# A two-layer decoder trunk on one core: scores negated as they are read, weight splits held back, first FFN sums ahead of splits

## The chip, the cores and the metric

The kernel runs on one NeuronCore of a Trainium2 chip. Its engines work side by side, each through its own queue in order: TensorE (PE, with its weight loads shown as PEld), VectorE (DVE), ScalarE (ACT), GpSimd (POOL) and SyncE (SP), which here only issues loads. The metric is device time in microseconds (us) of one launch. The order in each queue is fixed when the program is built: the builder lets a simulated clock run and gives each engine, at each moment, the earliest written instruction that is ready by that clock. On the chip an engine then takes its list from the front, and waits where the front is not ready.

## The reference

Two layers; each is half-step SwiGLU, token mixing, half-step SwiGLU, all on x of 256 rows and 1024 columns in float32, and a last RMS norm. Cut to what matters:

```python
def swiglu(x, w_gate, w_up, w_down):
    return (jax.nn.silu(x @ w_gate) * (x @ w_up)) @ w_down      # D_FF = 2816

def masked_softmax(s, valid):
    s = jnp.where(valid, s.astype(jnp.float32), NEG)
    m = jnp.max(s, axis=-1, keepdims=True)
    p = jnp.where(valid, jnp.exp(s - m), 0.0)
    return p / jnp.maximum(jnp.sum(p, axis=-1, keepdims=True), 1.0)

for l in range(DEPTH):                                           # DEPTH = 2
    x = x + 0.5 * swiglu(rms_norm(x, norm_ffn1[l]), ...)
    x = x + hybrid_mixer(rms_norm(x, norm_mix[l]), ...)          # 8 NSA heads, 8 MoBA heads
    x = x + 0.5 * swiglu(rms_norm(x, norm_ffn2[l]), ...)
return rms_norm(x, norm_final)
```

At 256 rows every block of keys is chosen, so each NSA head needs two softmaxes over causal scores (selected and window keys) and one over 15 compressed keys, and each MoBA head one.

## The kernel before, in words

**Exact products.** Every weight is used as two numbers, hi and lo, with hi + lo the float32 weight, and x likewise. Weights come as a stream of blocks of 128 x 1024, in the order of use (class `Stream`). SP loads a block into one of 5 raw buffers (`wraw`, line 236); ScalarE casts it to `whi` (line 260); VectorE subtracts to `wlo` (line 290). That is a *split*. There are 7 buffers for split blocks, freed when the last matmul of a block is done. A raw buffer is free, and SP's next load can start, when its `wlo` is written.

**When splits are written.** `split(n)` writes n of them if buffers are free; `pump()` writes splits until only `st.reserve` of the 7 buffers are left. `use()` takes the next block. Since the builder gives an engine whatever is ready first, `st.behind["V"]` and `st.behind["A"]` name an instruction of VectorE or ScalarE behind which all splits written from then on have to stand on that engine (`queue`, with `tc.issue_after`).

**FFN.** 22 blocks j of 128 hidden columns. For each, 8 pairs of matmuls for the gate and 8 for the up product (`wide`, lines 594 and 596: the first of a pair reads `whi`, the second `wlo`) go to two PSUM banks: tag B (two banks) for even j, C and D for odd j. `read(j)` (line 676) takes both banks: ScalarE copies one half of a bank (line 680), VectorE adds the other (line 681); then the bank is free. `finish(j)` multiplies by the norm's scale on GpSimd (line 689), applies silu on ScalarE, multiplies again on GpSimd (line 691), and splits the result. Down products (lines 572 to 574) follow later. At the start of an FFN (but for the first one) j = 0 and j = 1 are computed together (`gu_two`), then `read(0)`, `read(1)` and `st.split(2)` are written, then j = 2, which needs the B banks again. There are three such starts. When the matmuls of j = 0 and 1 begin, their four blocks hold four of the 7 buffers, and the blocks of j = 2 and 3 are the next to be split.

**Mixer.** Projections run as blocks `mk`, `mq` (two for each half of the MoBA heads), `mv` and `out`; `m_feat`, `m_v` and `part` use one block each and pump. Between them stand the heads' softmaxes. `nsa_s(h)` computes scores in PSUM (line 1101), and `softmax` reads them: for each of two branches VectorE scales, masks and stores the scores and reduces them to their maximum in one instruction (lines 1046, 1047; the accumulator read behind it writes `mx`), one small VectorE instruction turns the sign (`nm`, line 1049), and ScalarE computes the exponentials with `nm` as bias and their sums (lines 1051, 1052). `normalize` takes the reciprocals on VectorE and multiplies P on GpSimd (lines 1066, 1067); `nsa_t` turns P on TensorE (line 1074, into tag A) and ScalarE copies it out (`PT`, line 1076); `nsa_pv` multiplies by the values (line 1084). MoBA heads go the same way with one branch. The keys' and queries' rotation runs over ScalarE (line 820), two small transfers, VectorE and GpSimd (lines 826, 827); `m_stack` splits the turned keys (`KM`, line 1163).

Of the kernel before, what the change touches and what calls it, by code (L numbers as in the profile page):

```python
# [21 lines left out]
F32 = mybir.dt.float32  # L22
# [3 lines left out]
AF = mybir.ActivationFunctionType  # L26
OP = mybir.AluOpType
AX = mybir.AxisListType

D, S, L, DH = 1024, 256, 2, 64  # L30
# [51 lines left out]
def all_units(phases):  # L82
    return [u for ph, l in phases for u in phase_units(ph, l)]
# [234 lines left out]
def trunk(ctx, tc, xin, wst, w1st, gains, glast, cst, small, out, phases=PHASES, n_raw=5, n_hl=7):  # L318
    nc = tc.nc
    V, A, G, T = nc.vector, nc.scalar, nc.gpsimd, nc.tensor  # L320
# [3 lines left out]
    mp = ctx.enter_context(tc.tile_pool(name="mix", bufs=1))  # L324
# [3 lines left out]
    st = Stream(nc, wst, all_units(phases), rawp, hlp, n_raw, n_hl)  # L328
# [10 lines left out]
    def bank(tag):  # L339
        return ps.tile([128, 512], F32, name="ps" + tag, tag="ps" + tag, bufs=BUFS[tag])  # L340
# [24 lines left out]
    def con(n):  # L365
        a, c = CONST_AT[n]
        return cs_t[:, a:a + c]
# [27 lines left out]
    def half_of(h):  # L395
        return slice(h * 512, (h + 1) * 512)
# [18 lines left out]
    def x_add(h, o):  # L415
# [5 lines left out]
        for t in range(2):  # L421
            q = mp.tile([128, 512], F32, name="sqt", tag="P", bufs=3)
            A.activation(q, X[:, t, half_of(h)], AF.Square, accum_out=state["sq"][:, h, t:t + 1])
# [24 lines left out]
    def x_start_squares():  # L448
        sq = state["sq"] = mp.tile([128, 2, S], F32, name="sqacc", tag="P", bufs=3)
        with tc.issue_after(state["second_hi"]):  # L450
            A.activation(sq, XF[:, :2], AF.Square)
            for d in range(2, KT, 2):
                q = mp.tile([128, 2, S], F32, name="sqt", tag="P", bufs=3)
                A.activation(q, XF[:, d:d + 2], AF.Square)
                G.tensor_add(sq, sq, q)
        G.tensor_add(sq[:, 0], sq[:, 0], sq[:, 1])
# [6 lines left out]
    def last_add(t, n, o):  # L463
# [6 lines left out]
        V.tensor_add(x, x, o)  # L470
        q = mp.tile([128, 512], F32, name="sqt", tag="P", bufs=3)
        A.activation(q[:, :b - a], x, AF.Square, accum_out=sq[:, t, n:n + 1])
# [171 lines left out]
    def ffn(pi, name, l):  # L644
# [31 lines left out]
        def read(j):  # L676

            s = S_[j] = mp.tile([128, 2, S], F32, name="hs", tag="PT", bufs=5)
            for i, o in enumerate(pend.pop(j)):
                A.copy(s[:, i], o[:, S:])  # L680
                V.tensor_add(s[:, i], s[:, i], o[:, :S])  # L681

        def finish(j):
            n = 0 if j == NJ - 1 else 1
# [15 lines left out]
        def evac(j):  # L700
            read(j)
            finish(j)
# [101 lines left out]
    def mixer(pi, l):  # L804
# [95 lines left out]
        rotk = rawk[:, 2:4]  # L900
        rs = state["rs"]
        rs8 = mp.tile([128, 2], F32, name="rs8", bufs=2)
        nrs = mp.tile([128, 2], F32, name="nrs", bufs=2)
        G.tensor_scalar(rs8, rs, DH ** -0.5, None, op0=OP.mult)
        A.activation(warm, rs8[:, 0:1], AF.Exp, scale=0.0)
        G.tensor_scalar(nrs, rs, -1.0, None, op0=OP.mult)
# [86 lines left out]
        def c_scores():  # L993
            b = bank("A")
            for blk in range(2):
                for r in range(4):
                    c = (blk * 4 + r) * 32
                    T.matmul(b[:, c:c + 32], rawq[:, r, blk * 128:(blk + 1) * 128], KC, start=True, stop=True)
            P = mp.tile([128, 2, 8, 16], F32, name="Pc", bufs=1)
            m = mp.tile([128, 2, 8], F32, name="mc", bufs=1)  # L1000
            for blk in range(2):
                V.scalar_tensor_tensor(P[:, blk], b[:, blk * 128:(blk + 1) * 128].rearrange("p (h n) -> p h n", h=8),
                                       rs8[:, blk:blk + 1],
# [32 lines left out]
        m0, m1 = con("mask")[:, 128:], con("mask")  # L1036

        def softmax(key, s1, s0, nb, gates):

            P = mp.tile([128, 3, 2, 128], F32, name="P", tag="P", bufs=3)[:, :, :nb]  # L1040
            m = mp.tile([128, 2, nb], F32, name=f"mx{nb}", bufs=3)
            nm = mp.tile([128, 2, nb], F32, name=f"nm{nb}", bufs=3)
            sm = mp.tile([128, 2, nb], F32, name=f"sm{nb}", bufs=3)
            mk = m1.rearrange("p (k t) -> p k t", k=2)
            for r in range(nb):
                V.tensor_tensor_reduce(P[:, 0:2, r], s1[:, :, r], mk, rs8[:, 1:2], -3e38, OP.add, OP.max, m[:, 0, r:r + 1])
                read = V.tensor_tensor_reduce(P[:, 2, r], s0[:, r], m0, rs8[:, 0:1], -3e38, OP.add, OP.max,
                                              m[:, 1, r:r + 1]).ins
            V.tensor_scalar(nm, m, -1.0, None, op0=OP.mult)
            for r in range(nb):  # L1050
                A.activation(P[:, 0:2, r], P[:, 0:2, r], AF.Exp, bias=nm[:, 0, r:r + 1], accum_out=sm[:, 0, r:r + 1])
                e = A.activation(P[:, 2, r], P[:, 2, r], AF.Exp, bias=nm[:, 1, r:r + 1], accum_out=sm[:, 1, r:r + 1]).ins
            if gates is not None:
                st.behind["A"] = e
            PR[key] = (P, sm, nb, gates)
            return read
# [12 lines left out]
        def transpose_p(key, tag):  # L1069
            P, _, nb, _ = PR.pop(key)  # L1070
            for r in range(nb):
                b = bank(tag)
                for o, s in ((0, 2), (1, 0), (2, 1)):
                    last = T.transpose(b[:, o * 128:(o + 1) * 128], P[:, s, r], ident).ins
                t = mp.tile([128, 384], F32, name="PT", tag="PT", bufs=5)
                cur["copied"] = A.copy(t, b[:, :384]).ins
                PT[key, r] = t
            return last
# [30 lines left out]
        def nsa_t(h):  # L1109
            transpose_p(h, "A")  # L1110
# [23 lines left out]
        def m_feat(which, i):  # L1134
            if i == 0:
                cur["rot"] = RW("rot" + which)
            if i % 2 == 0:
                cur["b"] = bank("A")
            cur["last"] = feature_one(cur["b"][:, (i % 2) * S:(i % 2 + 1) * S], st.use("in", l, i), i % 2 == 0)
            if i % 2 == 1:  # L1140
                h = i // 2
                raw = mp.tile([128, 2, S], F32, name="mraw", tag="F", bufs=2)
                tabs = (CK, SK) if which == "mk" else (con("C"), con("Sg"))
                sw, ro = SW[:, 2 * h:2 * h + 2], cur["rot"][:, 2 * h:2 * h + 2]
                rope_begin(cur["b"], raw, sw, ro, tabs[0])
                ends.append((which, h, sw, ro, tabs[1]))
            st.pump()
# [90 lines left out]
        normalize(5)  # L1238
        m_end()
        nsa_s(6)  # L1240
        st.reserve = 2
        m_feat("mq", 2)
        nsa_pv(1)
        nsa_t(4)
# [1 line left out]
        m_stack()  # L1246
        nsa_s(7)
        nsa_t(5)
        m_feat("mq", 3)


# [55 lines left out]
        nsa_t(6)  # L1307
        normalize(("m", 0))
        moba_s(1)
        st.reserve = 1  # L1310
        st.behind.clear()
        m_v(1)
        nsa_t(7)
# [12 lines left out]
                 (moba_s, 7), (part, 3, 0), (normalize, ("m", 6)), (moba_pv, 2), (part, 3, 1), (moba_t, 6), (part, 4, 0),  # L1326
                 (normalize, ("m", 7)), (moba_t, 7), (part, 4, 1), (moba_pv, 3)]
        for f, *args in steps:
            if args == [4, 0]:
                st.reserve = 0  # L1330
            with tc.issue_after(last):
                last = f(*args) or last
        st.reserve = 1
# [30 lines left out]
    for pi, (ph, l) in enumerate(phases):  # L1364
        if ph == "mix":
            mixer(pi, l)
        else:
            ffn(pi, ph, l)
# [36 lines left out]
```

## Time and profile before

| | us |
|---|---|
| median of three runs (1019.35 to 1098.41) | 1021.62 |
| profiled execution | 1018.07 |
| its span, first to last instruction | 1016.3 |
| PE busy in it | 996.7 (98%) |
| DVE busy | 698.2 (69%) |
| ACT busy | 592.6 (58%) |
| POOL busy | 323.0 (32%) |

The mean granted clock of TensorE was 0.997 of full speed. The first mixer runs from about 191 to 322 us, the second from about 691 to 821; the three FFN starts in question lie at about 338, 523 and 837 us. Read the table for how little room each engine leaves, and then the stages one by one: a share of the whole span hides that VectorE is nearly full in the middle of a mixer.

### The profile page before, as it was taken

Reading aid. Unit: us, or ns where it says so; the run is one execution under the profiler, and the core shown is the slowest. Engines: PE = TensorE matmul, PEld = TensorE weight load, DVE = VectorE, ACT = ScalarE, POOL = GpSimd, SP = SyncE. Lnnn points to the kernel's source line nnn. Section 1 sums busy time; section 2 is a strip of 40 time slices with the busy share of each in tenths; the row PEclk is TensorE's granted clock in tenths of the full one; section 3 lists DMA queues with packets and bytes.
Section 4 is the critical chain, followed back from the end, with each engine's and each line's share of the span. In section 5 each row is a group of like instructions: output and inputs, shape, how many; then the busy total and the mean of one; then the engine's idle time right before and its main releaser. Section 6 shows DMA issues by size and latency. Waiting matters only on the chain.

```text
span 1016.3 us, 16192 instructions
## 1 busy us (share of the span) xinstructions
PE 996.7 (98%) x5873; PEld 861.8 (85%) x5873; DVE 698.2 (69%) x1195; ACT 592.6 (58%) x1137; POOL 323.0 (32%) x412
## 2 busy tenths in 40 slices
PE   9999999999899999999999999999999999999997
PEld 7888888899778888888888888889987788888885
DVE  6876566689984866666676656666899757666664
ACT  6755555557864855555575555456578756555552
POOL 2322122136751322222242222131477313222220
PEclk9999999999999999999999999999999999999999
DMA  8786776354452666666557677863436427666631
GB/s 275 249 292 198 266 251 214 105 171 149 130 166 84 213 205 193 195 188 189 164 186 207 188 232 231 280 189 125 158 110 185 132 84 252 198 212 187 189 123 42
DMA packets 52848, 188.21 MB, mean 185 GB/s; under 512 B 6368, under 2 KB 6752, under 8 KB 51616
## 3 DMA queue, kind: packets, MB, share of 16 engines
q1 hardware_dynamic: 49680, 182.17, 56.5%
q10 hardware_dynamic: 3088, 5.01, 1.8%
q8 instruction: 46, 0.75, 0.3%
q14 instruction: 34, 0.28, 0.1%
HBM read 182.04 MB, written 1.05 MB: 180 GB/s over the span
## 4 chain that ended last, share of the span: by engine, by line
PE 91%; DVE 4%; ACT 2%; issue 1%; POOL 1%; DMA 1%; ACTq 0%; POOLq 0%; DVEq 0%
PE psB L594 16%; PE psA L572 9%; PE psA L574 9%; PE psA L573 9%; PE psB L596 8%; PE psC L594 8%; PE psD L594 8%; PE psD L596 4%; PE psC L596 4%; PE psA L565 2%; PE psA L566 2%; PE psA L567 2%; PE psA L407 1%; PE psD L1084 1%; DVE wlo L290 1%
## 5 line engine op out<-in xcount | busy, mean ns | idle before, releaser
L290 DVE TENSOR_TENSOR wlo<-wraw,whi 128x1024 fp32r<-128x1024 f32 x325 | 411.1, 1272 | 208.7 <-ACT whi L260 208.3
L260 ACT CAST whi<-wraw 128x1024 fp32r<-128x1024 f32 (+1 forms) x326 | 337.7, 1044 | 276.3 <-issue 172.1
L594 PE MATMUL psB<-x,whi 128*128 128x512 f32 x688 | 242.4, 393 | 1.1 <-DVE hs L681 1.1
L689 POOL TENSOR_TENSOR hs<-hs,rbc 128x256 f32<-128x256 f32 x88 | 76.5, 871 | 400.7 <-DVE hs L681 366.5
L596 PE MATMUL psB<-x,wlo 128*128 128x256 f32 x688 | 192.6, 280 | 0.0
L594 PEld LDWEIGHTS psB<-x,whi 128*128 128x128 f32 x688 | 129.2, 188 | 30.0 <-DVE hs L681 1.9
L574 PE MATMUL psA<-wlo,hp 128*128 128x512 f32 (+1 forms) x356 | 137.6, 387 | 0.0
L573 PE MATMUL psA<-whi,hp 128*128 128x512 f32 (+1 forms) x356 | 137.5, 387 | 0.0
L572 PE MATMUL psA<-whi,hp 128*128 128x512 f32 (+1 forms) x356 | 137.0, 388 | 0.5 <-DVE X L470 0.5
L596 PEld LDWEIGHTS psB<-x,wlo 128*128 128x128 f32 x688 | 129.4, 188 | 1.4
L691 POOL TENSOR_TENSOR hs<-hs,rbc 128x256 f32<-128x256 f32 x88 | 101.8, 1160 | 72.2 <-ACT hs L690 72.0
L594 PE MATMUL psC<-x,whi 128*128 128x512 f32 x344 | 122.0, 392 | 0.0
L594 PE MATMUL psD<-x,whi 128*128 128x512 f32 x344 | 121.7, 391 | 0.0
L596 PE MATMUL psC<-x,wlo 128*128 128x256 f32 x344 | 96.2, 280 | 0.0
L596 PE MATMUL psD<-x,wlo 128*128 128x256 f32 x344 | 96.2, 280 | 0.0
L572 PEld LDWEIGHTS psA<-whi,hp 128*128 128x128 f32 x356 | 66.8, 188 | 14.3 <-DVE X L470 0.7
L574 PEld LDWEIGHTS psA<-wlo,hp 128*128 128x128 f32 x356 | 66.8, 188 | 13.7
L573 PEld LDWEIGHTS psA<-whi,hp 128*128 128x128 f32 x356 | 66.9, 188 | 12.2
L594 PEld LDWEIGHTS psD<-x,whi 128*128 128x128 f32 x344 | 64.6, 188 | 14.3
L594 PEld LDWEIGHTS psC<-x,whi 128*128 128x128 f32 x344 | 64.6, 188 | 14.1
L565 PE MATMUL psA<-x,whi 128*128 128x256 f32 x256 | 73.0, 285 | 0.0
L567 PE MATMUL psA<-x,wlo 128*128 128x256 f32 x256 | 72.3, 282 | 0.0
(245 smaller groups left out, 1599.8 us busy)
## 6 DMA issues: line engine op xcount, KB each, us to landing
wraw<-in_w SPq DMA_DIRECT2D x318, 512.0 KB, 4.3
W1a<-in_w SPq DMA_DIRECT2D x4, 1024.0 KB, 6.2
W1mixn<-in_w SPq DMA_DIRECT2D x2, 1024.0 KB, 6.4
W1late<-in_w SPq DMA_DIRECT2D x2, 1024.0 KB, 5.9
KM<-KM ACTq DMA_DIRECT2D x8, 256.0 KB, 3.8
wraw<-in_w SPq DMA_DIRECT2D x4, 420.0 KB, 3.1
wraw<-in_w SPq DMA_DIRECT2D x4, 256.0 KB, 4.8
X<-in_small SPq DMA_DIRECT2D x1, 1024.0 KB, 7.3
```

Of the source, the lines that this page charges most:

```text
L260: self.last_hi = self.nc.scalar.copy(hi[:, a:b], raw[:, a:b]).ins
L290: eng.tensor_sub(lo[:, :c], raw[:, :c], hi[:, :c].bitcast(F32))
L565: T.matmul(o, hi, xh, start=first, stop=False, skip_group_check=True)
L566: T.matmul(o, hi, xl, start=False, stop=False, skip_group_check=True)
L567: return T.matmul(o, lo, xh, start=False, stop=last, skip_group_check=True).ins
L572: T.matmul(o, parts[:, 0, c], hi, start=first, stop=False, skip_group_check=True)
L573: T.matmul(o, parts[:, 1, c], hi, start=False, stop=False, skip_group_check=True)
L574: return T.matmul(o, parts[:, 0, c], lo, start=False, stop=last, skip_group_check=True).ins
L594: T.matmul(o, blk128(hi, k), x.rearrange("p a t -> p (a t)"), start=k == 0, stop=k == KT - 1, skip_group_check=True)
L596: last = T.matmul(o[:, S:], blk128(lo, k), x[:, 0], start=False, stop=k == KT - 1, skip_group_check=True).ins
L689: G.tensor_mul(g, g, state["rbc"])
L691: G.tensor_mul(g, g, state["rbc5"])
```

## The change

Three parts. The score scale is negated (a new small tile `nrs8`, one GpSimd instruction per mixer), the reduction takes the minimum, so that it writes minus the maximum, and the exponential takes scale -1; the 32 `nm` instructions go. The reserve of split buffers stays 3 through the block `mq 2` instead of `mk 3`; in the `mv` blocks it stays 2, and in the output product it falls from 2 to 1 to 0 at parts 0, 2 and 4, where before it was 1 from the second `mv` block and 0 from part 4. And in every FFN but the first, the splits written behind `read(0)` stand behind its second sum on VectorE.

```diff
--- before.py
+++ after.py
@@ -678,7 +678,9 @@
             s = S_[j] = mp.tile([128, 2, S], F32, name="hs", tag="PT", bufs=5)
             for i, o in enumerate(pend.pop(j)):
                 A.copy(s[:, i], o[:, S:])
-                V.tensor_add(s[:, i], s[:, i], o[:, :S])
+                add = V.tensor_add(s[:, i], s[:, i], o[:, :S]).ins
+            if j == 0 and pi > 0:
+                st.behind["V"] = add
 
         def finish(j):
             n = 0 if j == NJ - 1 else 1
@@ -900,7 +902,9 @@
         rotk = rawk[:, 2:4]
         rs = state["rs"]
         rs8 = mp.tile([128, 2], F32, name="rs8", bufs=2)
+        nrs8 = mp.tile([128, 2], F32, name="nrs8", bufs=2)
         nrs = mp.tile([128, 2], F32, name="nrs", bufs=2)
+        G.tensor_scalar(nrs8, rs, -DH ** -0.5, None, op0=OP.mult)
         G.tensor_scalar(rs8, rs, DH ** -0.5, None, op0=OP.mult)
         A.activation(warm, rs8[:, 0:1], AF.Exp, scale=0.0)
         G.tensor_scalar(nrs, rs, -1.0, None, op0=OP.mult)
@@ -1037,19 +1041,21 @@
 
         def softmax(key, s1, s0, nb, gates):
 
+
             P = mp.tile([128, 3, 2, 128], F32, name="P", tag="P", bufs=3)[:, :, :nb]
-            m = mp.tile([128, 2, nb], F32, name=f"mx{nb}", bufs=3)
             nm = mp.tile([128, 2, nb], F32, name=f"nm{nb}", bufs=3)
             sm = mp.tile([128, 2, nb], F32, name=f"sm{nb}", bufs=3)
             mk = m1.rearrange("p (k t) -> p k t", k=2)
             for r in range(nb):
-                V.tensor_tensor_reduce(P[:, 0:2, r], s1[:, :, r], mk, rs8[:, 1:2], -3e38, OP.add, OP.max, m[:, 0, r:r + 1])
-                read = V.tensor_tensor_reduce(P[:, 2, r], s0[:, r], m0, rs8[:, 0:1], -3e38, OP.add, OP.max,
-                                              m[:, 1, r:r + 1]).ins
-            V.tensor_scalar(nm, m, -1.0, None, op0=OP.mult)
+                V.tensor_tensor_reduce(P[:, 0:2, r], s1[:, :, r], mk, nrs8[:, 1:2], 3e38, OP.add, OP.min,
+                                       nm[:, 0, r:r + 1])
+                read = V.tensor_tensor_reduce(P[:, 2, r], s0[:, r], m0, nrs8[:, 0:1], 3e38, OP.add, OP.min,
+                                              nm[:, 1, r:r + 1]).ins
             for r in range(nb):
-                A.activation(P[:, 0:2, r], P[:, 0:2, r], AF.Exp, bias=nm[:, 0, r:r + 1], accum_out=sm[:, 0, r:r + 1])
-                e = A.activation(P[:, 2, r], P[:, 2, r], AF.Exp, bias=nm[:, 1, r:r + 1], accum_out=sm[:, 1, r:r + 1]).ins
+                A.activation(P[:, 0:2, r], P[:, 0:2, r], AF.Exp, scale=-1.0, bias=nm[:, 0, r:r + 1],
+                             accum_out=sm[:, 0, r:r + 1])
+                e = A.activation(P[:, 2, r], P[:, 2, r], AF.Exp, scale=-1.0, bias=nm[:, 1, r:r + 1],
+                                 accum_out=sm[:, 1, r:r + 1]).ins
             if gates is not None:
                 st.behind["A"] = e
             PR[key] = (P, sm, nb, gates)
@@ -1238,7 +1244,6 @@
         normalize(5)
         m_end()
         nsa_s(6)
-        st.reserve = 2
         m_feat("mq", 2)
         nsa_pv(1)
         nsa_t(4)
@@ -1246,6 +1251,7 @@
         m_stack()
         nsa_s(7)
         nsa_t(5)
+        st.reserve = 2
         m_feat("mq", 3)
 
 
@@ -1307,7 +1313,6 @@
         nsa_t(6)
         normalize(("m", 0))
         moba_s(1)
-        st.reserve = 1
         st.behind.clear()
         m_v(1)
         nsa_t(7)
@@ -1326,8 +1331,8 @@
                  (moba_s, 7), (part, 3, 0), (normalize, ("m", 6)), (moba_pv, 2), (part, 3, 1), (moba_t, 6), (part, 4, 0),
                  (normalize, ("m", 7)), (moba_t, 7), (part, 4, 1), (moba_pv, 3)]
         for f, *args in steps:
-            if args == [4, 0]:
-                st.reserve = 0
+            if f is part and args[0] in (0, 2, 4) and args[1] == 0:
+                st.reserve = 2 - args[0] // 2
             with tc.issue_after(last):
                 last = f(*args) or last
         st.reserve = 1
```

## Rows read from the trace of the kernel before

**Rows 1.** The page, busy us per engine (share of the span) and instructions.
```profile
PE 996.7 (98%) x5873; PEld 861.8 (85%) x5873; DVE 698.2 (69%) x1195; ACT 592.6 (58%) x1137; POOL 323.0 (32%) x412
```
**Rows 2.** Waits of TensorE: who waited for whom: us in total, times, longest us.
```profile
PE psA L1074 <- POOL P L1067: 6.1, 7, 2.1
PE psA L1074 <- ACT PT L1076: 2.2, 2, 1.1
PE psB L594 <- DVE hs L681: 1.1, 2, 0.6
...
PE psB L1275 <- DVE mx L1047: 0.5, 1, 0.5
...
PE psD L1084 <- ACT PT L1076: 0.5, 1, 0.5
```
**Rows 3.** Windows, first mixer: from:to, busy us (instructions) per engine, PEclk, DMA share, GB/s.
```profile
218.50:320.00 101.50, 96.38 (x693) 81.09 (x692) 84.48 (x218) 72.33 (x186) 56.08 (x72) 0.98 0.48 143
```
**Rows 4.** Timeline of TensorE, first mixer: start us, us, what, [idle before <-releaser].
```profile
259.05 0.52 PE L1074 MATMUL psA<-const,P 128*128 128x128 f32 x3 [1.10 <-ACT PT L1076]
...
270.63 0.55 PE L1074 MATMUL psA<-const,P 128*128 128x128 f32 x3 [2.15 <-POOL P L1067]
...
272.99 0.55 PE L1074 MATMUL psA<-const,P 128*128 128x128 f32 x3 [1.34 <-POOL P L1067]
```
**Rows 5.** Windows, behind the third gap.
```profile
272.00:278.00 6.00, 5.01 (x21) 4.35 (x22) 5.05 (x13) 4.56 (x16) 4.56 (x9) 0.72 0.68 200
```
**Rows 6.** Timeline of GpSimd, head of the first mixer.
```profile
199.03 0.21 POOL L904 TENSOR_SCALAR rs<-ny 128x2 f32<-128x2 f32 x1
```
**Rows 7.** Groups of VectorE: what, times, busy us, mean ns of one, idle before.
```profile
L1049 DVE TENSOR_SCALAR nm<-mx 128x4 f32<-128x4 f32 (+1 forms) x32 | 9.1, 283 | 0.3
...
L1046 DVE DVE_READ_ACCUMULATOR2_ANT mx<- 128x1 f32 x48 | 3.9, 81 | 0.0
```
**Rows 8.** Waits of all engines, the row of ScalarE for nm.
```profile
ACT P L1051 <- DVE nm L1049: 20.0, 17, 2.2
```
**Rows 9.** Timeline of ScalarE, first mixer.
```profile
254.69 0.51 ACT L1051 ACTIVATE P<-P,nm 128x256 f32<-128x256 f32 x1 [0.95 <-DVE nm L1049]
...
258.42 0.86 ACT L1076 COPY PT<-psA 128x384 f32<-128x384 f32 x2
```
**Rows 10.** Timeline of VectorE, first mixer.
```profile
265.17 2.27 DVE L290 TENSOR_TENSOR wlo<-wraw,whi 128x1024 fp32r<-128x1024 f32 x1
...
270.21 1.45 DVE L290 TENSOR_TENSOR wlo<-wraw,whi 128x1024 fp32r<-128x1024 f32 x1
271.58 1.09 DVE L1163 TENSOR_TENSOR KM<-rotmq,KM 64x512 fp32r<-64x512 f32 x1
```
**Rows 11.** The page's DMA issues: KB each, median us from issue to landing.
```profile
wraw<-in_w SPq DMA_DIRECT2D x318, 512.0 KB, 4.3
```
**Rows 12.** Timeline of VectorE, start of the FFN behind the first mixer.
```profile
333.26 4.63 DVE L290 TENSOR_TENSOR wlo<-wraw,whi 128x1024 fp32r<-128x1024 f32 x4 [0.46 <-ACT whi L260]
337.81 0.41 DVE L681 TENSOR_TENSOR hs<-hs,psB 128x256 f32<-128x256 f32 x1
```
**Rows 13.** Timeline of TensorE, the same FFN start.
```profile
338.28 0.50 PE L594 MATMUL psB<-x,whi 128*128 128x512 f32 x1 [0.56 <-DVE hs L681]
338.61 0.28 PE L596 MATMUL psB<-x,wlo 128*128 128x256 f32 x1
```
**Rows 14.** Timeline of ScalarE, the same FFN start.
```profile
336.50 0.39 ACT L680 COPY hs<-psB 128x256 f32<-128x256 f32 x1
336.76 1.07 ACT L260 CAST whi<-wraw 128x1024 fp32r<-128x1024 f32 x1
337.71 0.40 ACT L680 COPY hs<-psB 128x256 f32<-128x256 f32 x1
```
**Rows 15.** Timeline of GpSimd, first mixer.
```profile
266.43 2.16 POOL L827 TENSOR_TENSOR rotmq<-rotmq,SW 128x512 f32<-128x512 f32 x1
```
**Rows 16.** Instructions on tile rbc: duration ns min/median/max, first and last start us.
```profile
L689 POOL TENSOR_TENSOR hs<-hs,rbc x88: 728/853/1722, 37.7 to 992.2; 128x256 f32<-128x256 f32 x88
```

## The prediction

> **What bounds the kernel now.** I read the page's first part to see which engine fills the span, then the waits of TensorE to see what its gaps wait for, then the timeline of each engine around the gaps that the change touches. TensorE (PE) is busy 996.7 of 1016.3 us [rows 1]: all its gaps together are 19.6 us, so this change, which takes no matmul away, cannot gain 2% (20.4 us). What is to be seen in the waits [rows 2]: the gaps that count are few and short. Seven waits of the transposes for GpSimd's product P (6.1 us), two for a ScalarE copy PT (2.2), two of the first wide matmul of an FFN for VectorE's sum hs (1.1), and single ones (0.5 each). The mixers hold most of it: in the first, PE is busy 96.38 of 101.5 us and VectorE 84.48 [rows 3]. [...] The second mixer has the same order of work and shorter gaps.
>
> **The change, part by part.** The sum is made against the profiled execution, 1018.07 us (span 1016.3 and 1.8 around it). The median of the runs shown, 1021.62, is 3.6 above that; the lowest, 1019.35, is 1.3 above.
>
> **nrs8.** One GpSimd instruction in each mixer, 0.21 us like its neighbour [rows 6]. It stands where PE runs matmuls that need no scale; I take 0. Without that cover it would be 2 x 0.21 = 0.4.
>
> **nm.** The sign operation goes: 32 VectorE instructions, together 9.1 us [rows 7]. VectorE is no bound over the span, so the 9.1 are not the gain; what counts is that ScalarE's exponentials waited for nm 17 times, 20.0 us in all [rows 8]. Only where such a wait reaches PE is there anything to win. That is one place in each mixer: at 254.69 the exponentials of one head start after ScalarE idled 0.95 us for nm, which GpSimd's work had stretched to over 1 us; they, a copy and four casts run without a gap up to the PT copies at 258.42 [rows 9], and those are what PE waits 1.10 us for [rows 4]. Without nm that chain starts 0.95 earlier. Then GpSimd's product is late next, so the other gaps stay. I take -0.95 in each mixer, -1.9. Ends: 0, if ScalarE puts other work there, and -2.2, both waits.
>
> **min.** Instead of max, with scale -1 in the exponential. No row shows a min reduction. The nearest is the max one with the same operands, so I take 0. The far end is another accumulator read of 0.08 us [rows 7] behind each of the 20 reductions (five heads of four) in the stretch of each mixer where the gaps lie: 2 x 20 x 0.08 = +3.2. Below nothing, because the same elements are read.
>
> **Reserve.** Followed in order, the reserve does this: at the block mq 2 one block is split instead of two, and the second comes after mq 3; from mv 1 to out 7 each split comes one block later; from the first FFN block on all is as before. No split is added or left out. The one that moves at mq 2 is the VectorE split at 270.21 (1.45 us) [rows 10] with its ScalarE cast. It lies beside the second product of the head on which the 1.34 us gap waits. But K's two subtractions of 1.1 us follow it on VectorE [rows 10] and move up into its place, so I count a third: -0.4 in each mixer, -0.8. For the later ones, the two waits of 0.5 [rows 2] lie right behind a cast or a split: I take half, -0.5. Ends: 0, and all of the waits for P and the two 0.5, -7.1. The clock drop I leave as it is: the gaps ahead of it shrink by 0.4 of 3.5 us. Its end is -1.7. On the SP queue the loads of the held blocks follow one block later; they land in 4.3 us [rows 11], while one block lasts PE 2.7 us and four are held, so nothing waits.
>
> **First sums.** Reading them ahead of the splits adds a wait, at three FFN starts (all but the first). Before, VectorE split four blocks in one piece, 333.26 to 337.89, and added the first sum at 337.81 [rows 12]; PE, done with its work at 337.72, waited 0.56 for it [rows 13]. Now all splits of that stage stand behind the second sum. That sum needs ScalarE's second copy, and ScalarE's order holds the copies behind its own casts, which the change does not touch: cast, copy 336.50, cast 336.76, copy 337.71 to 338.11 [rows 14]. So VectorE stands still from 332.8 until the first copy; the second sum runs 338.15 to 338.5, the first split of 4.63 / 4 = 1.16 [rows 12] ends at 339.7. PE gets its bank earlier, but its second matmul reads that split; before, it ran at 338.61 [rows 13]. So PE is 1.1 later: +1.1 at each start, +3.3. The gap that is named in the trace goes, and the split is late next. Queued behind the wait are the other splits and, through the freed buffers, SP's loads: about 5 us later. The sixth block is cast only when its load has landed, 339.7 + 4.3 = 344, and split by 347; PE comes to it after five blocks of 2.7 us, at 353. That cover is 6 us, so 0. Ends: if the copies come ahead of the casts, both sums end by 336.5, the split by 337.7, and two waits of 0.56 go, -1.1; on the other side, below, +7.
>
> **Contention.** In the first mixer a split beside GpSimd's rotation took 2.27 us and the rotation 2.16 [rows 10, 15]; the four splits ran at 1.16 each. So the two hold each other up, and a split that moves next to GpSimd's first FFN product can be held too. The product takes 0.73 to 1.72 us, median 0.85 [rows 16]. In my order the first sum ends at 337.3 (336.89 and 0.41), its product at 338.2, ahead of the split, so I take 0. [...]
>
> Sum: 1018.07 - 1.9 - 0.8 - 0.5 + 3.3 = 1018.2. I forecast **1018 us, no change**: the mixers give 3.2 back, the FFN starts take 3.3.
>
> **The rivals.** Early sums. If ScalarE's order turns so that copies precede casts, the starts give -1.1: 1018.2 - 3.3 - 1.1 = 1013.8. For it: ScalarE is free of dependences there. Against: both orders are made before the run, and nothing that ScalarE waits for changes.
>
> Split behind the product (slower). If VectorE takes the third sum ahead of the first split (+0.4, its length in [rows 12]) then GpSimd's product of it is issued just ahead of the split and holds it 0.85 [rows 16]. That is 1.25 more at three starts, +3.8: 1022.0. It decides where the third copy ends before the second sum does, that is where ScalarE lags by 0.4 us; the copy of the third bank follows the second directly, so it is close. Its far end is every start at both the longest product and the fourth sum, 1.72 + 0.8 = 2.5, +7.
>
> Empty mixers. The order of work there is made anew, and the wait for nm becomes one for GpSimd's product, whose engine is full in the same stretch: 1018.1 + 3.3 = 1021.4.
>
> No effect of the edge: the change does not do what it says. The edge behind the sum orders nothing that was in the way, and the starts stay as they are: 1018.1 - 3.2 = 1014.9. The splits at 333.26 do come from calls behind the sum, which speaks against it.
>
> **How the numbers follow.** Forecast 0.45, early sums 0.20, split behind product 0.14, empty mixers 0.16, no effect of the edge 0.05. The range goes from 1012 (early sums and the clock drop gone: 1013.8 - 1.7) to 1025 (the product rival with most of the min reduction's end, 1022.0 + 3.2); beyond lie 2 in 10. The forecast's own range is 1015 to 1021: the 3.2 of the mixers doubled or at none. A measurement of this kernel tells about 2% from no change. Faster by that needs all of PE's gaps: 0.01. Slower needs +20, nearly three times the worst end at the starts: 0.02. Within: 0.97.
>
> **What would show it.** Right: no nm rows; the wait of P for nm gone and PE's wait for PT near 0.1; at the FFN starts the row for hs gone from PE's waits and one for wlo in its place, some 2 us at two starts and 1.3 at the third; the clock of the first mixer still low for some 3 us. Wrong: hs copies ahead of the casts on ScalarE, a wlo wait under 0.5, or new gaps for P in the mixers beyond 3.5 us each.

## The result, and the profile after

The changed kernel took **1014.0 us** (median of 5 runs, 1012.77 to 1015.1) beside 1019.35 for the kernel before in the same session: a ratio of 0.9948, 95% interval 0.9925 to 0.9971. One of the five runs of the kernel before took 1098.41 us, far outside the others, so the second measurement, beside 19 runs of before ("changed, again" in the table below: 0.9968), is the firmer one. The forecast was 1018, no change. The time lies inside its range of 1012 to 1025, but 1.0 below the forecast's own 1015 to 1021. The profiled execution took 1014.0 with a span of 1012.0, against 1018.07 and 1016.3.

The page of the changed kernel (its first part, as [rows 1]) and its waits of TensorE (as [rows 2]; us in total, times, longest):

```profile
PE 994.7 (98%) x5873; PEld 861.0 (85%) x5873; DVE 692.7 (68%) x1163; ACT 592.5 (59%) x1137; POOL 320.3 (32%) x414
```
```profile
PE psA L1187 <- DVE rotmq L825: 2.8, 2, 1.4
PE psB L596 <- DVE wlo L290: 1.9, 3, 0.6
PE psB L594 <- DVE hs L681: 1.3, 2, 0.7
PE psA L1080 <- POOL P L1073: 1.2, 2, 0.6
```

VectorE lost its 32 instructions. Waits for P fell from 6.1 to 1.2 us and the wait for PT of 2.2 is gone. Two new rows of some size stand in: `rotmq`, which the prediction did not have, and `wlo`, which it had.

The windows of the changed kernel (as [rows 3, 5]) and its waits of ScalarE for nm (as [rows 8]):

```profile
218.50:320.00 101.50, 99.07 (x717) 83.91 (x716) 80.69 (x206) 74.34 (x193) 53.79 (x71) 1.00 0.48 144
...
272.00:278.00 6.00, 6.00 (x30) 4.91 (x29) 5.69 (x7) 3.61 (x10) 6.00 (x5) 1.00 1.00 298
```
```profile
ACT P L1055 <- DVE nm L1050: 3.9, 12, 0.6
ACT P L1057 <- DVE nm L1052: 3.6, 4, 1.2
```

PE is busy 2.7 us more of the same stretch of time, and the clock no longer falls (1.00 where it was 0.72). The exponentials wait 7.5 us instead of 20.0.

TensorE's timeline of the changed kernel: the gaps of the first mixer (as [rows 4]), the first two of the three FFN starts (as [rows 13]), and the four small matmuls of L547 that each of these three FFNs issues soon after its beginning:

```profile
256.12 0.85 PE L1080 MATMUL psA<-const,P 128*128 128x128 f32 x6 [0.15 <-DVE rotmq L825]
...
264.08 0.48 PE L1109 MATMUL psC<-KK,qs 128*128 128x256 f32 x2 [0.24 <-DVE sm L1066]
...
266.25 0.55 PE L1080 MATMUL psA<-const,P 128*128 128x128 f32 x3 [0.63 <-POOL P L1073]
...
271.09 0.47 PE L1187 MATMUL psA<-whi,x 128*128 128x512 f32 x1 [1.41 <-DVE rotmq L825]
...
326.72 0.60 PE L547 MATMUL psA<-const,ny 128*128 128x128 f32 x4
...
332.71 0.40 PE L594 MATMUL psB<-x,whi 128*128 128x512 f32 x1
333.76 0.50 PE L594 MATMUL psB<-x,whi 128*128 128x512 f32 x1 [0.65 <-DVE hs L681]
334.89 0.39 PE L596 MATMUL psB<-x,wlo 128*128 128x256 f32 x1 [0.63 <-DVE wlo L290]
...
512.88 0.60 PE L547 MATMUL psA<-const,ny 128*128 128x128 f32 x4
...
520.36 0.39 PE L596 MATMUL psB<-x,wlo 128*128 128x256 f32 x1 [0.64 <-DVE wlo L290]
...
825.38 0.60 PE L547 MATMUL psA<-const,ny 128*128 128x128 f32 x4
```

The gaps of the first mixer sum to 2.4 us; before they were 5.0, with one of 0.41 ahead of the three of [rows 4]. L547 makes a good ruler, since PE's work between two of them is the same in all kernels. An idle row understates a stall, here by 0.17: it counts from the end that the profile models for the matmul ahead of it (the one at 332.71 is drawn 0.40 us long), while matmuls of this kind are followed by the next after 0.23 where PE does not wait. Before, the three rows of L547 were:

```profile
331.57 0.60 PE L547 MATMUL psA<-const,ny 128*128 128x128 f32 x4
...
516.62 0.60 PE L547 MATMUL psA<-const,ny 128*128 128x128 f32 x4
...
830.70 0.60 PE L547 MATMUL psA<-const,ny 128*128 128x128 f32 x4
```

The table gives the stretches that these rows cut from the span, worked out the same way for every kernel, each from one profiled execution; the ratios are from all its runs. FFN 1, 2 and 3 are the FFNs of the three starts. "To FFN 1" holds all ahead of the first of them, with the first mixer; "1 to 2" one FFN start; "2 to 3" one start and the second mixer; "to end" one start.

| kernel | to FFN 1 | 1 to 2 | 2 to 3 | to end | span | ratio, 95% interval |
|---|---|---|---|---|---|---|
| before | 331.57 | 185.05 | 314.08 | 185.60 | 1016.3 | |
| changed | 326.72 | 186.16 | 312.50 | 186.62 | 1012.0 | 0.9948 [0.9925, 0.9971] |
| changed, again | 327.11 | 186.16 | 312.49 | 186.64 | 1012.4 | 0.9968 [0.9957, 0.9979] |
| no hold | 326.92 | 185.05 | 311.52 | 185.51 | 1009.0 | 0.9934 [0.9922, 0.9946] |
| hold only | 329.95 | 186.16 | 314.89 | 186.70 | 1017.7 | 1.0046 [1.0030, 1.0062] |
| negation only | 329.79 | 185.05 | 312.79 | 185.57 | 1013.2 | 0.9977 [0.9965, 0.9990] |
| reserve only | 330.64 | 185.06 | 316.03 | 185.57 | 1017.3 | 0.9985 [0.9970, 0.9999] |
| hold at third split | 326.74 | 184.36 | 311.37 | 184.83 | 1007.3 | 0.9921 [0.9908, 0.9934] |
| hold at fourth sum | 327.84 | 186.79 | 313.08 | 187.29 | 1015.0 | 0.9999 [0.9988, 1.0010] |
| negation, mq half | 326.79 | 185.05 | 311.60 | 185.56 | 1009.0 | 0.9939 [0.9925, 0.9952] |
| negation, later half | 329.50 | 185.10 | 312.72 | 185.58 | 1012.9 | 0.9972 [0.9959, 0.9985] |
| third split, reserve 4 | 324.96 | 184.36 | 310.00 | 184.88 | 1004.2 | 0.9882 [0.9866, 0.9897] |
| no hold, 32 unread | 325.89 | 185.05 | 309.68 | 185.58 | 1006.2 | 0.9881 [0.9861, 0.9901] |
| third split, 32 unread | 324.90 | 184.36 | 309.70 | 184.84 | 1003.8 | 0.9872 [0.9856, 0.9889] |

So the time came from the mixers and part of it went at the starts: changed against no hold, the starts cost 1.11, 0.98 and 1.11, together 3.2 us; no hold against before, the mixers give 4.65 and 2.56, together 7.2.

The first column is the least firm. Up to that row "before" and "hold only" have the same instructions in the same order on VectorE, ScalarE and GpSimd, and still differ by 1.62; so do "changed", "changed, again" and "hold at fourth sum", which differ by up to 1.12, and the two with 32 unread instructions, by 0.99. The stretch "1 to 2" agrees to 0.05 wherever the hold is the same.

### The profile page after: what moved, and what is told of

It is laid out like the page before. It is cut to its first block, busy times and chain, and to the rows that moved or that the text cites. A ratio compares the mean times of both kernels' runs of the same rounds, so it can differ in the third digit from the quotient of the medians.

```text
span 1012.0 us, 16119 instructions
## 1 busy us (share of the span) xinstructions
PE 994.7 (98%) x5873; PEld 861.0 (85%) x5873; DVE 692.7 (68%) x1163; ACT 592.5 (59%) x1137; POOL 320.3 (32%) x414
## 4 chain that ended last, share of the span: by engine, by line
PE 92%; ACT 4%; DVE 2%; issue 1%; DMA 1%; ACTq 0%
PE psB L594 15%; PE psA L572 9%; PE psA L574 9%; PE psA L573 9%; PE psB L596 8%; PE psC L594 7%; PE psD L594 7%; PE psC L596 4%; PE psD L596 4%; PE psA L567 3%; PE psA L565 3%; PE psA L566 3%; ACT whi L260 1%; PE psD L1090 1%; PE psA L1187 1%; PE psA L407 1%
## 5 line engine op out<-in xcount | busy, mean ns | idle before, releaser
L573 PE MATMUL psA<-whi,hp 128*128 128x512 f32 (+1 forms) x356 | 137.5, 387 | 0.0
L572 PE MATMUL psA<-whi,hp 128*128 128x512 f32 (+1 forms) x356 | 134.1, 388 | 0.5 <-DVE X L470 0.5
```

Of the source, the lines that this page charges most:

```text
L572: T.matmul(o, parts[:, 0, c], hi, start=first, stop=False, skip_group_check=True)
L573: T.matmul(o, parts[:, 1, c], hi, start=False, stop=False, skip_group_check=True)
```

## The experiments

**The parts alone.** Three kernels run one part each, and one runs the change without the hold:

```diff
--- changed kernel, without the hold
-            if j == 0 and pi > 0:
-                st.behind["V"] = add
--- negation only: also the reserve put back
         nsa_s(6)
+        st.reserve = 2
         m_feat("mq", 2)
...
-        st.reserve = 2
         m_feat("mq", 3)
...
         moba_s(1)
+        st.reserve = 1
...
-            if f is part and args[0] in (0, 2, 4) and args[1] == 0:
-                st.reserve = 2 - args[0] // 2
+            if args == [4, 0]:
+                st.reserve = 0
```

*No hold.* Expected: 

> The changed kernel without the hold: the splits of an FFN start are free to run ahead of the first sums, as before; negation and reserve stay. Theory A (the hold costs: at the three starts PE waited 0.56, 0 and 0.55 us before and 1.28, 0.64 and 1.29 after): 2.1 us faster than the changed kernel, about 1012, ratio to before 0.993; the three waits for hs and wlo go back to 0.56, 0 and 0.55. Theory B (the hold removes the wait that the trace names and so saves 1.1): 1.1 slower than the changed kernel, 1015, ratio 0.996.

Measured: 1010.81 us beside 1017.98. Against the changed kernel's two measurements the hold costs 1.4 and 3.4 thousandths, and 3.2 us by the table; the mixers keep their gain. Theory A had the direction, and with 2.1 too small a price, as it counted idle rows alone.

*Hold only.* Expected: 

> The kernel before with the hold alone. Theory A: 2.1 us slower than before, ratio 1.002, PE's waits at the three starts 1.3, 0.6 and 1.3, the mixers as before (gaps of 5.0 and 4.3 us, clock drop of 1.7 in the first). Theory B: 1.1 faster, ratio 0.999.

Measured: 1022.7 us, +4.7. Start to start it adds the same 1.11 (1 to 2) and 1.10 (to end). Its median lies 3.2 above its own profiled run, whose first mixer is 1.6 shorter than before's; what the median adds beyond the starts is in no trace, and the shorter first mixer is no gain of the edit, which changes no order there.

*Negation only.* Expected: 

> The kernel before with the negated scores alone (no nm; reserve and FFN starts as before). Theory C (the mixers gained by nm's absence: exponentials start at once, so softmaxes come earlier all along): most of the 6.2 us, -4 to -6, ratio 0.995, PE's waits for P and PT in the mixers from 8.4 to under 4 us and no clock drop. Theory D (as predicted, nm is worth one wait of 0.95 in each mixer): -1.9, ratio 0.998, the waits for P of 6.1 us and the clock drop stay.

Measured: 1015.21 us, -2.3 by the ratio. That is Theory D's number, and the clock drop stays as it said, but the waits are as Theory C said: those for P and PT go as in the full change, but a longer gap takes their place. TensorE's gaps there, and VectorE's queue ahead of the first one:

```profile
272.84 1.19 PE L1279 MATMUL psB<-KM,qs 128*128 128x256 f32 x4 [2.63 <-DVE nm L1050]
...
771.97 0.71 PE L1279 MATMUL psB<-KM,qs 128*128 128x256 f32 x4 [2.64 <-DVE nm L1050]
```
```profile
269.24 2.77 DVE L290 TENSOR_TENSOR wlo<-wraw,whi 128x1024 fp32r<-128x1024 f32 x2
271.94 0.47 DVE L1048 CUSTOM_DVE_ANT_0 P<-psB,const,nrs 128x256 f32<-128x256 f32 x1
...
272.61 0.68 DVE L823 TENSOR_TENSOR rotmq<-psA,const 128x512 f32<-128x512 f32 x1
```

Two splits stand ahead of the reduction and of the read of the turned queries. In the changed kernel it is one (VectorE, the same place):

```profile
268.71 1.23 DVE L290 TENSOR_TENSOR wlo<-wraw,whi 128x1024 fp32r<-128x1024 f32 x1
269.85 0.48 DVE L1050 CUSTOM_DVE_ANT_0 P<-psB,const,nrs 128x256 f32<-128x256 f32 x1
...
270.25 0.69 DVE L825 TENSOR_TENSOR rotmq<-psA,const 128x512 f32<-128x512 f32 x1
```

*Reserve only.* Expected: 

> The kernel before with the held-back reserve alone. Theory C: -0.5 to -1.5 us, ratio 0.999, the large gaps for P stay. Theory E (the gain came from the splits taken out of VectorE's full stretch): -3 to -5, ratio 0.996, the waits for P from 6.1 to 2 us or less and no clock drop. As predicted: -1.3.

Measured: 1016.24 us, -1.5 by the ratio, as Theory C and the prediction said. Without the negation the waits for P stay (7.3 us, the longest 2.8). In this execution the clock fell in the second mixer too: 0.80 from 740 to 750 us, 0.86 in the ten after. The longest idle row of that stretch is shorter than the 1.41 of the changed kernel:

```profile
744.97 0.55 PE L1074 MATMUL psA<-const,P 128*128 128x128 f32 x3 [1.20 <-POOL P L1067]
```

By the ratios the parts alone give -2.3 and -1.5, together -6.7 (no hold); each of the three is sure to 1.2 to 1.5 us either way. The next two kernels show where the extra 2.9 comes from.

**Which half of the reserve.** To the negation one half of the reserve is added, without the hold:

```diff
--- negation with the mq half: against negation only
-        st.reserve = 2
         m_feat("mq", 2)
...
+        st.reserve = 2
         m_feat("mq", 3)
--- negation with the later half: against negation only
-        st.reserve = 1      # at moba_s(1)
...
+            if f is part and args[0] in (0, 2, 4) and args[1] == 0:
+                st.reserve = 2 - args[0] // 2
```

*mq half.* Expected: 

> The kernel before with the negated scores and only the first half of the held-back reserve (one split fewer at mq 2, one more at mq 3; from mv 1 on as before; no hold). Theory G (the two help each other: with nm gone the last gap of the head stage waits for the split that the reserve takes away): the gap of 2.63 us goes to 1.4 in both mixers, no clock drop in the first, all of the gain of both together, ratio 0.993 to 0.994. Rival H (it is the later half, in the mv and out blocks): as with the negation alone, 0.998, gaps of 2.6 and the clock drop stay.

Measured: 1010.82 us, equal to no hold. *Later half.* Expected: 

> The kernel before with the negation and only the later half of the reserve (2 until part 2 of the output product, 1 from there, 0 at part 4), with the mq half and the FFN hold left as before. Theory G (the split at mq 2 alone makes the difference between the parts tried singly and together): as the negation alone, ratio 0.998, a gap of about 2.6 us in each mixer at the keys' matmul remains, and the granted clock of the first mixer stays low at 270 to 280 us (near 0.83). Rival (the later half frees VectorE too): ratio 0.995 to 0.996 and one of the gaps is shorter.

Measured: 1015.67 us beside 1018.3, equal to the negation alone; gaps of 2.6 and a clock of 0.83 (270 to 280) remain. So the one split withheld at mq 2 makes the whole difference, as Theory G said, and by the table it can be followed to the end: from negation only to the mq half the first mixer gains 329.79 - 326.79 = 3.00 and the second 312.79 - 311.60 = 1.19. The gap shrinks from 2.63 to 1.41, that is 1.22, one split (1.23 above). In the second mixer that is all. In the first, in these executions, the clock adds (1 - 0.83) x 10 = 1.7; 1.22 + 1.7 = 2.9. The windows of negation only, 270 to 280 and the same place of the second mixer (PEclk is the third figure from the end), show it:

```profile
270.00:280.00 10.00, 7.37 (x29) 6.00 (x29) 8.18 (x15) 5.51 (x14) 9.48 (x12) 0.83 0.87 245
770.00:780.00 10.00, 8.03 (x39) 6.32 (x41) 7.32 (x14) 5.19 (x12) 9.41 (x10) 1.00 0.98 288
```

**Where the hold should stand.** The changed kernel again; the hold placed behind the first two splits, on both engines; and the hold moved one block further (`j < 2`):

```diff
--- hold at third split: against the changed kernel
-                A.copy(s[:, i], o[:, S:])
+                cp = A.copy(s[:, i], o[:, S:]).ins
...
-            if j == 0 and pi > 0:
-                st.behind["V"] = add
+            if j == 0:
+                state["first"] = {"A": cp, "V": add}
...
                 st.split(2)
+                if pi > 0:
+                    st.low()
+                    st.behind.update(state["first"])
```

(`st.low()` writes the VectorE half of the split that is still open.) *Changed, again.* Expected: 

> The changed kernel as it is, once more, beside the next ones on the same chip. Ratio to before 0.995, between the runs of its parts: if the hold costs 2.1 us, it lies 0.002 above the kernel without the hold (0.9934) and the sum of its gaps at the three starts is 3.2 us.

Measured: 1014.17 us beside 1017.73, 0.0034 above no hold instead of 0.002. *Third split.* Expected: 

> The changed kernel with the hold put behind the first two splits of a start (the blocks of j = 2) and on ScalarE too, so that ScalarE's first two copies come ahead of its third cast. Theory A (the cost comes from the first split being late, and that from ScalarE's casts ahead of its copies): PE's gaps at all three starts go to under 0.1 us, 3.2 us less than the changed kernel and 1.1 less than the one without the hold: ratio 0.992, about 1010. Rival F (ScalarE's order does not matter; the sums are late because PE's products end late): gaps of 0.5 us or more stay at two starts, no faster than without the hold.

Measured: 1009.11 us. Its ScalarE now copies before it casts, and VectorE takes two splits, both sums, and then the rest:

```profile
329.81 0.38 ACT L680 COPY hs<-psB 128x256 f32<-128x256 f32 x1
330.85 0.38 ACT L680 COPY hs<-psB 128x256 f32<-128x256 f32 x1 [0.66 <-PE psB L596]
331.12 2.95 ACT L260 CAST whi<-wraw 128x1024 fp32r<-128x1024 f32 x3
```
```profile
328.43 2.36 DVE L290 TENSOR_TENSOR wlo<-wraw,whi 128x1024 fp32r<-128x1024 f32 x2 [0.45 <-ACT whi L260]
330.71 0.96 DVE L681 TENSOR_TENSOR hs<-hs,psB 128x256 f32<-128x256 f32 x2
332.20 3.50 DVE L290 TENSOR_TENSOR wlo<-wraw,whi 128x1024 fp32r<-128x1024 f32 x3 [0.53 <-ACT whi L260]
```

No wait for hs or wlo is left at any start, as Theory A said: 0.7 us less than no hold at the first and the third. Against the changed kernel of the same session it gains 5.1, where Theory A had 3.2: the stretches of its starts give 1.8, 1.1 and 1.8 by the table, more than their idle rows. *Fourth sum.* Expected: 

> The changed kernel with the hold behind the fourth sum instead of the second. Theory A: the first split starts two sums (2 x 0.33 us) later, so PE's wait for wlo is 0.7 longer at each of three starts: +2.0 us, ratio 0.997. Rival F (the hold itself costs nothing, the difference seen lies elsewhere): no change, 0.995.

Measured: 1017.31 us, 3.1 more than the changed kernel. By the table, beside "changed, again", 1.9 of that lies at the starts (0.63, 0.59 and 0.65), close to Theory A's 2.0. The 0.7 to 1.1 ahead of the first start is a difference between executions: the order on VectorE, ScalarE and GpSimd is the same there in all three traces. Two more sums stand ahead of the first split (2 x 0.33), and that split itself is held, as its GpSimd and VectorE rows show:

```profile
335.24 0.74 POOL L691 TENSOR_TENSOR hs<-hs,rbc 128x256 f32<-128x256 f32 x1 [0.81 <-DVE hs L681]
```
```profile
334.75 0.41 DVE L681 TENSOR_TENSOR hs<-hs,psC 128x256 f32<-128x256 f32 x1
335.08 0.41 DVE L681 TENSOR_TENSOR hs<-hs,psD 128x256 f32<-128x256 f32 x1
335.41 7.26 DVE L290 TENSOR_TENSOR wlo<-wraw,whi 128x1024 fp32r<-128x1024 f32 x5
```

PE's first matmul on that split runs at 337.12, 1.71 after the split began; in the changed kernel it was 1.27 (333.62 to 334.89). The 0.44 between them is near what was left of the product when the split began (335.98 - 335.41 = 0.57).

**The gap that is left.** One more block withheld at mq 2, on top of the hold at the third split:

```diff
         nsa_s(6)
+        st.reserve = 4
         m_feat("mq", 2)
...
-        st.reserve = 2
         m_feat("mq", 3)
+        st.reserve = 2
```

Expected: 

> The changed kernel with the hold behind the third split, and the reserve at 4 through mq 2 and at 2 only behind mq 3, so that one more split leaves VectorE ahead of the turned query rotmq. Theory (the 1.4 us gap left in each mixer is a wlo split standing ahead of rotmq): the gap falls to about 0.3 in each mixer, so 2.2 us less than with the hold alone: ratio near 0.990, about 1007. Rival (the reduction of the next head takes the free place on VectorE, or the splits that come later make a new wait): as with the hold alone, ratio 0.992, or a new row for wlo among TensorE's waits.

Measured: 1006.36 us beside 1018.3. PE waits 0.79 and 0.80 for rotmq instead of 1.41, and the wait for P of 0.63 is gone: 2 x (0.62 + 0.63) = 2.5 of the 3.1 us of span. The first of the two:

```profile
269.29 0.50 PE L1190 MATMUL psA<-whi,x 128*128 128x512 f32 x1 [0.79 <-DVE rotmq L828]
```

The theory had the time, not its parts. The gap fell by less than expected: PE goes on 1.77 us earlier (269.29 against 271.06 in the kernel without the reserve of 4), but it also comes to the place 1.15 earlier.

**What the sign instruction had cost.** Without the hold, 32 VectorE instructions are put back, which write a tile that nobody reads:

```diff
+            dm = mp.tile([128, 2, nb], F32, name=f"dm{nb}", bufs=3)
...
+            V.tensor_scalar(dm, nm, -1.0, None, op0=OP.mult)
```

Expected: 

> The changed kernel without the hold, with 32 small VectorE instructions put back that turn the sign of nm into a tile that nobody reads: VectorE works as much as before, but no exponential waits for it. Theory C (the negation gains because ScalarE's exponentials no longer stand behind that instruction): as without them, ratio 0.993 to 0.995, the two gaps at the turned queries stay near 1.4 us and the first mixer's clock at 1.00. Rival V (the gain is VectorE's time and places in its queue, in the stretch where it is nearly full): 0.996 to 0.999, with gaps for GpSimd's P or VectorE's queue of 2 us or more back in the mixers.

Measured: 1006.74 us beside 1018.51, a ratio of 0.9881 where the kernel without them has 0.9934. Neither theory had that. They take as long as nm did [rows 7], and in no hold there is nothing in their place:

```profile
L1053 DVE TENSOR_SCALAR dm<-nm 128x4 f32<-128x4 f32 (+1 forms) x32 | 9.5, 298 | 0.2
```

The builder's simulated clock goes by other instructions now, and it writes another order. TensorE's timeline of this kernel at the place of the gap, and VectorE's read:

```profile
268.86 0.55 PE L1080 MATMUL psA<-const,P 128*128 128x128 f32 x3 [0.35 <-POOL P L1073]
269.16 0.83 PE L1281 MATMUL psB<-KM,qs 128*128 128x256 f32 x5
269.83 0.39 PE L1187 MATMUL psA<-whi,x 128*128 128x512 f32 x1
```
```profile
275.24 0.68 DVE L823 TENSOR_TENSOR rotmq<-psA,const 128x512 f32<-128x512 f32 x1
```

The value projection (L1187) starts at 269.83 although VectorE reads rotmq 5.4 us later: what it had waited for was no data (it reads `whi` and x), but one of the four banks of tag A. Rival V's forecast failed: with VectorE's 9.5 us put back nothing of the gain was lost. But Theory C is not shown by it either. The order of the queues is another one, so the run cannot tell what the negation alone gains by, and that stays argued. Some 5 thousandths came with the new order, more than either part of the change gave alone; which of the 32 instructions turned it stays open.

*Third split with the 32.* Expected: 

> The hold behind the third split together with the 32 small instructions that nobody reads. Theory O (the small instructions only set another order in the mixers, and the hold only another order at the FFN starts, so the two add up): 1.3 to 1.8 us less than the small instructions alone, ratio 0.986 to 0.987, no wait of TensorE for hs or wlo at the starts and no gap over 0.5 us in either mixer. Rival (each placement sets the order of everything behind it, so the gain in the mixers does not carry over): 0.990 to 0.993, with the gaps of 1.4 us back.

Measured: 1005.32 us beside 1017.63. No idle row above 0.44 is left in either mixer, and none for hs or wlo at the starts. The two orders add up, as Theory O said: the median is 1.4 us below that of the 32 alone, and by the table the stretches with the first and the third start are 0.69 and 0.74 shorter. (The 0.99 of the first column is a difference between executions, see above.) This one, the 32 alone and the reserve of 4 are the fastest versions, 0.9872 to 0.9882; the intervals don't tell them apart.

## Why the prediction was right or wrong, step by step

**The bound** held: PE is busy 994.7 us, and no version reached 2%, since its gaps were all there was.

**First sums** held to a tenth: +3.3 forecast, 3.2 measured, by the step that was named: PE's first matmul on a late `wlo`, with the sums read in ScalarE's old order. From the ruler's row to that matmul it was 7.04 us before (331.57 to 338.61 [rows 13]) and is 8.17 now (326.72 to 334.89), 1.13 more. ScalarE, VectorE and GpSimd at the first start, changed kernel (as [rows 12, 14]):

```profile
330.71 1.05 ACT L260 CAST whi<-wraw 128x1024 fp32r<-128x1024 f32 x1
331.64 0.39 ACT L680 COPY hs<-psB 128x256 f32<-128x256 f32 x1
331.90 1.07 ACT L260 CAST whi<-wraw 128x1024 fp32r<-128x1024 f32 x1
332.85 0.40 ACT L680 COPY hs<-psB 128x256 f32<-128x256 f32 x1
```
```profile
332.06 0.42 DVE L681 TENSOR_TENSOR hs<-hs,psB 128x256 f32<-128x256 f32 x1 [4.10 <-ACT hs L680]
333.28 0.42 DVE L681 TENSOR_TENSOR hs<-hs,psB 128x256 f32<-128x256 f32 x1 [0.80 <-ACT hs L680]
333.62 4.03 DVE L290 TENSOR_TENSOR wlo<-wraw,whi 128x1024 fp32r<-128x1024 f32 x3
```
```profile
332.56 0.73 POOL L691 TENSOR_TENSOR hs<-hs,rbc 128x256 f32<-128x256 f32 x1 [6.42 <-DVE hs L681]
```

VectorE stands still 4.10 us for the copies. The product ends at 333.29, before the split: contention 0 held here. The idle rows came out otherwise than the signs said: the row for hs did not go, since PE waits for the first sum too (0.65), and those for wlo are 0.63 to 0.64 at each start instead of some 2 and 1.3. Early sums, at 1013.8, names nearly the time that came, but that is luck, since it did not happen: the copies stayed behind the casts. Only the kernels with the hold at the third split made that order, and two of the starts then gave 0.7 each.

**Split behind the product** did not happen in the changed kernel, whose first split follows a finished product; two sums later it does (hold at fourth sum). That split's reader starts 1.71 us after it, against 1.27 behind a finished product: 0.44 more, where the rival's estimate was the product's whole 0.85. The rival's far end, three times 2.5, is 7.6 and not 7. The example in "Contention" is told loosely, too: the rotation of 2.16 began 1.26 us behind the start of the split of 2.27, while the GpSimd product ahead of it began 0.10 us before the split (GpSimd, kernel before):

```profile
265.07 1.28 POOL L826 TENSOR_TENSOR SW<-SW,SK 128x512 f32<-128x512 f32 x1 [4.43 <-DMA SW<-mraw]
```

This ended at 266.35, the split at 267.44 [rows 10], the rotation at 268.59 [rows 15]: each of the two later ones ends 1.1 to 1.2 us behind the one that began before it. That the product and not the rotation lengthened the split is argued from these ends.

**min** is worth 0, as taken: VectorE's two kinds of reduction took 475 and 343 to 346 ns on the mean with the maximum and 481 and 346 with the minimum, and the accumulator reads 81 and 83. **nrs8** was not run apart.

**nm** and **reserve**, each by itself, came close: -1.9 forecast and -2.3 measured, -1.3 and -1.5. The nm of its chain took 1.25 us (from 253.41; the median of the 32 is 0.17), beside a GpSimd rotation of 1.35 from 253.28, as said. But the nm step was half right in its mechanism. The PT wait went, as said; "the other gaps stay" did not, as the waits for P fell too, from 6.1 to 1.3 us, and a gap of 2.6 came. The later half of the reserve (-0.5) showed nothing beyond the noise: 0.9972 against 0.9977, and no hold and mq half are equal to 0.01 us.

**The step that failed** is "The clock drop I leave as it is", with the reserve's "so I count a third" ahead of it. The drop is the 0.72 of [rows 5], and its 1.7 us, which the low end of the range takes whole, are (1 - 0.72) x 6; the clock stood at 0.50 of full speed from 274 to 277 us, and in the changed kernel at 1.00. I priced the two parts one by one in the queues of before. Where both are made, one whole split leaves VectorE ahead of the reader that PE waits for, the gap is 1.41 instead of 2.63, and in every profiled execution with that gap the clock held (1.00 from 268 to 280 us). By the table the mixers' 7.2 us are 3.1 for the negation alone (1.78 and 1.29), 2.4 for a split in each, 1.7 for the clock; I had 1.9, 1.3 and 0. That is the whole miss of 4 us. These terms are not equally sure. The split's 1.2 stands in both mixers of four traces (a gap of 2.63 in negation only and in the later half, of 1.41 in no hold and in the mq half). The clock's 1.7 is seen in the same traces, but that the shorter gap is what kept the clock up is argued: the reserve alone had a drop behind an idle row of 1.20, and negation only had none behind 2.64. The 1.78 of the negation is hardly more than the 1.62 by which two executions of the same order differ. The mq half without the negation was not run by itself; reserve only, which holds it, gave 1.5. The negation by itself moves more than 0.95 us of waiting, because the order is made anew. GpSimd's rotation, which stood at 266.43 and took 2.16 [rows 15], ran in negation only as

```profile
262.16 1.36 POOL L827 TENSOR_TENSOR rotmq<-rotmq,SW 128x512 f32<-128x512 f32 x1
```

**Empty mixers** had named that remaking of the order, with the wrong sign. **No effect of the edge** was refuted by the 1.1 at each start.

## What to carry to other kernels

In a kernel whose queues are ordered by a simulated clock, two small edits near one place need not add: run each alone and both together. Here the interaction, 2.9 us, was larger than either part, 2.3 and 1.5. A wait of the bound engine that names a small reader can be a long instruction of another stream queued ahead of that reader: here it was a split ahead of the read of rotmq, holding one back took 1.22 us off the gap, and a second one took off another 0.62. Place an edge behind the work that the next consumer needs first: two splits, then the sums, then the rest gains 0.7 at a start where the sums ahead of all splits lose 1.1. And take the same kernel's difference between two executions, up to 1.6 us in a stretch here, before a part of that size is called shown.

## What the runs showed of the hardware

TensorE's granted clock did not go by the length of a gap: in one execution of negation only, a gap of 2.63 us was followed by a clock of 0.83 over ten us, and one of 2.64 in the second mixer by 1.00. Reserve only fell to 0.80 in a stretch whose longest idle row is 1.20, while rows of 1.41 and 1.42 in the changed kernel were followed by 1.00. Nor is it the same each time: runs of the kernel before, in one session, went from 1014.77 us at a mean clock of 0.999 to 1021.47 at 0.993, while the kernel with the hold at the third split, with no gap over 1.41 in its mixers, stayed within 1008.96 to 1009.43 at 0.998 to 0.999. Most versions without longer gaps were as steady, but not all: the hold at the fourth sum, with the same 1.41, went from 1015.83 to 1019.44 at 0.999 to 0.996. Where its clock fell is in no trace.
